# One plain column instead of two ahead of the seven-product columns in an encoder's feed-forward

## The chip, the cores and the metric

The kernel runs on one core of a Trainium2 chip. The metric is device time in microseconds (us) of the whole program; the time before is 2812.5 us, the median of three runs. Five engines work side by side, each through its own fixed list of instructions: PE (TensorE, matrix products into PSUM banks), DVE (VectorE), ACT (ScalarE), POOL (GpSimd) and SP (SyncE, which here issues the data transfers).

## The reference, cut to what matters

A two-layer encoder trunk is applied to a prompt of 256 tokens and a sample of 1024 tokens, all in float32, with a model width of 1024. Each layer has a mixer and then a feed-forward network with 2816 hidden values:

```
for i in range(DEPTH):                       # DEPTH = 2
    ...                                      # mixer: y
    x = x + g1 * rms_norm(y, norm_g[i, 1])
    h = rms_norm(x, norm_g[i, 2]) * (1 + sc2) + sh2
    a, bb = jnp.split(h @ ffn_w_in[i], 2, axis=-1)
    y = (jax.nn.silu(a) * bb) @ ffn_w_out[i]
    x = x + g2 * rms_norm(y, norm_g[i, 3])
```

The change lies in `h @ ffn_w_in[i]`, the first product of the feed-forward, once per layer.

## The kernel before, in words

**Blocks and precision.** The tokens lie in three blocks: A and B (512 sample tokens each) and C (256 prompt tokens). A float32 product is made of three fast matmuls: each operand is split into a high and a low part (`hi`, `lo`), and hi·hi, hi·lo and lo·hi are summed in PSUM. `hhi` and `hlo` hold these parts of the block's normalised values h, transposed, in 8 slices of 128 features.

**A plain column.** The hidden values are made in 22 columns j of 128. In a plain column (`plain`, L1236, with `mm3`, L299) the a half and the b half of the column are products of 8 slices x 3 = 24 matmuls for each block. `L1241` takes silu of the a half on ACT, `L1243` multiplies by the b half on DVE.

**A seven-product column.** In the other columns (loop at L1274, `seven`, L1224) A and B are multiplied together by a Strassen-Winograd scheme: the four block products of (A, B) with (a, b) are made of seven products of half depth, 12 matmuls each, while C stays plain. It needs sums of the blocks, T2, T3 and T4, and sums of the column's weights. `combos` (L1160) makes the block sums: 16 subtractions on DVE (L1164), then 16 splits, each a cast on ACT (L1157) and a subtraction on DVE (L1158), in the order hhiA/hloA, T2, T3, T4. `sums` (L164; L169 to L172) makes the weight sums, four DVE operations per column, and `parts` (L141, L142) splits them. The weight sums lie in the first half of the tile `both` (L1271), a buffer in which the last input of T4 lies until then. The seven products come in this order: two of block B with the weights' a half; C; T2 with the weight sums; A with the weight sums; T3; C; T4; the second half of A. The product with T4 adds into the bank that the sum at L1307 on DVE reads first.

**What comes ahead.** The values h of a block come out of `boundary` (L484): the sums of squares of the product before, eight additions of the old x on DVE (L507) with x loaded in pieces by SP (L490) into three buffers and the result stored (L511), a second norm with its small DVE rows (L466 to L472), four scalings on DVE (L520), and then `turn` (L524): for each of 8 slices four transposes on PE (L532), the high part on ACT (L535), the value on ACT (L540) or DVE (L538), the low part on DVE (L542). The blocks come in the order C, A, B, and plain columns of a block stand between the boundaries of the next (L1251 to L1267).

**What sets the order.** The kernel keeps lists of side work (`vec`, `fill`) and takes from them at each `tick` by the microseconds that it reckons for the products just issued; `drain_with` and `vec.drain` empty a list. A layer below then gives each engine a fixed list. An engine works through its list in order and waits at an instruction until its inputs are there.

**After the columns of a pair.** `rights` (L1181) stores and combines the four blocks of a pair of columns for the second product (SP stores at L1183, sums at L1189 to L1197); `lefts` (L1204) does the same for the second product's weights, in the second half of `both`.

Of the kernel before, what the change touches and what calls it, by code (L numbers as in the profile page):

```python
# [8 lines left out]
F32 = mybir.dt.float32  # L9
# [20 lines left out]
ORDER = ["C", "A", "B"]  # L30
DRING = 5
VR = 1.2
NPL = 2
NK = NH // 2
RUNS = "1674253"

# [2 lines left out]
def encoder_kernel(  # L39
# [19 lines left out]
    def nm(s):  # L59
        uid[0] += 1  # L60
        return f"{s}_{uid[0]}"
# [127 lines left out]
    class Work:  # L189
# [8 lines left out]
        def tick(self, us):  # L198
            self.credit += us
            while self.q and self.credit > 0:  # L200
                try:
                    self.credit -= next(self.q[0])
                except StopIteration:
                    self.q.pop(0)
            if not self.q:
                self.credit = 0.0
# [10 lines left out]
    vec = Work()  # L217
    fill = Work()

    def drain_with(gen, other):  # L220
        while gen in vec.q:
            vec.tick(1.0)
            if other is not None:
                next(other, None)
# [5 lines left out]
    def cols(w, m, width=128, k0=0, kn=KD):  # L230
        v = w.rearrange("(k p) m -> p k m", p=128)
        return v[:, k0 : k0 + kn, m : m + width]

    def spec_cols(key, w, c0):
        units.specs.append((key, cols(w, c0), 128))
# [25 lines left out]
    def spec_ffn(L):  # L261
        wi, wo = ffn_w_in[L], ffn_w_out[L]
        for j in range(NPL):
            spec_cols(("a", L, j), wi, j * 128)
            spec_cols(("b", L, j), wi, HID + j * 128)
        for j in range(NPL, NH):
            pair = (cols(wi, j * 128), cols(wi, HID + j * 128))
# [321 lines left out]
    with tc.tile_pool(name="st", bufs=1, reuse_waits="tile") as st:  # L589
# [61 lines left out]
        class ADP:  # L651
            i = 0
# [419 lines left out]
    bt = ctx.enter_context(tc.tile_pool(name="bt", bufs=2, reuse_waits="tile"))  # L1072
# [11 lines left out]
    def ypart(blk, h, dt=F32, shape=None):  # L1084
        return yp.tile(shape or [128, 4 if blk != "C" else KD, BLK[blk]], dt, tag=f"y{blk}{h}", name=nm("y"))
# [66 lines left out]
    def ffn_in(L, gens_in, fp, t_in):  # L1152
# [7 lines left out]
        def combos():  # L1160
            a0, a1, b0, b1 = v_of["A"] + v_of["B"]
            for i in range(4):
                for out, x, y in ((b0, a0, b0), (a0, a1, a0), (a1, a1, b0), (b1, b1, a1)):
                    dve.tensor_sub(out[:, i, :], x[:, i, :], y[:, i, :])  # L1164
                    yield 0.7
            for i in range(4):
                split_t(b0, hhi["A"][:, i, :], hlo["A"][:, i, :], i)
                yield 0.7
            T[2] = ypart("B", 0, F32R), ypart("B", 1, F32R)
            T[3] = ypart("A", 0, F32R), fp.tile([128, 4, 512], F32R, tag="t4l", name=nm("t3"))  # L1170
            for n, t in ((2, a1), (3, a0)):
                for i in range(4):
                    split_t(t, T[n][0][:, i, :], T[n][1][:, i, :], i)
                    yield 0.7
            T[4] = tuple(fp.tile([128, 4, 512], F32R, tag=t, name=nm("t4")) for t in ("t3l", "t3h"))
            for i in range(4):
                split_t(b1, T[4][0][:, i, :], T[4][1][:, i, :], i)
                yield 0.7


        def rights(k, a, b, c, d):  # L1181
            def put(o, t):
                dma(out=td[o][:, k, :], in_=t)  # L1183

            yield 3.0
            for o, t in (("1", a), ("2", c), ("3", d)):
                put(o, t)
            x = bt.tile([128, 512], F32, tag="r", name=nm("x"))
            dve.tensor_sub(x, b, a)  # L1189
            yield 1.4  # L1190
            dve.tensor_sub(b, d, b)
            yield 1.4
            put("5", x)
            dve.tensor_add(a, b, a)
            yield 1.4
            put("7", b)
            dve.tensor_sub(c, a, c)  # L1197
            yield 1.4
            put("6", a)
            yield 1.4  # L1200
            put("4", c)


        def lefts():  # L1204
            w = ffn_w_out[L].rearrange("(k t p) (h c) -> k p t h c", t=2, p=128, h=2)
            for k in range(NK):
                for c0 in (0, 256):
                    t = both[:, 2:4, :].rearrange("p i (u c) -> p (i u) c", u=2)
                    for i in range(2):
                        dma(out=t[:, 2 * i : 2 * i + 2, :], in_=w[k][:, i, :, c0 : c0 + 256])  # L1210
                    yield 12.0
                    dve.tensor_add(t[:, 3, :], t[:, 1, :], t[:, 3, :])
                    dve.tensor_sub(t[:, 1, :], t[:, 0, :], t[:, 1, :])
                    yield 1.0
                    dve.tensor_sub(t[:, 0, :], t[:, 3, :], t[:, 0, :])
                    dve.tensor_sub(t[:, 2, :], t[:, 2, :], t[:, 0, :])
                    yield 6.0
                    dma(out=s_dr[L][:, k, :, c0 : c0 + 256], in_=t)
                    yield 1.0
# [16 lines left out]
        def plain(blk, j, w, part, s):  # L1236
            n = BLK[blk]
            ps = (ps_mm() if part == 0 or blk != "C" else ps_ax())[:, :n]
            mm3(ps, w, blk)
            if part == 0:  # L1240
                act.activation(s, ps, AF.Silu)  # L1241
            else:
                dve.tensor_mul(s, s, ps)  # L1243
                if blk == "C":
                    store_c(j, s)

        first = ypart("C", 0, F32, [128, 4, 512])
        place = {"A": first[:, 0:2, :], "B": first[:, 2:4, :]}

        ua, ub = [], []  # L1250
        for ib, blk in enumerate(ORDER):  # L1251
            us_ = 5.4 * BLK[blk] / 512
            drain_with(gens_in[blk], None)
            if blk == "B":
                vec.push(combos())
            for j in range(NPL):
                if ib == 0:
                    ua.append(units.next(("a", L, j), 2))
                    ub.append(units.next(("b", L, j), 1))
                if blk == "C":  # L1260
                    s = bt.tile([128, 256], F32, tag="accC", bufs=1, name=nm("gc"))
                else:
                    s = place[blk][:, j, :]
                plain(blk, j, ua[j], 0, s)
                tick(us_, 0.8)
                plain(blk, j, ub[j], 1, s)
                tick(us_, 0.8)  # L1267
        vec.push(rights(0, *(first[:, i, :] for i in (0, 2, 1, 3))))
        vec.drain()
        units.spare = lambda: ypart("C", 0, F32R, [128, 2, 1024])  # L1270
        both = ypart("A", 1)  # L1271
# [1 line left out]
        fill.push(lefts())  # L1273
        for j in range(NPL, NH):  # L1274
            last = j == NH - 1
# [52 lines left out]
            else:  # L1328
                even = ga, gb
# [135 lines left out]
    rights = Rights(0)  # L1465
    with tc.tile_pool(name="f0", bufs=1, reuse_waits="tile") as fp:
        gens = out_proj("go", 0, 0, fp)
        units.ahead(3)
        ffn_in(0, gens, fp, rights.upto)
# [200 lines left out]
    rights = Rights(1)  # L1670
    with tc.tile_pool(name="f1", bufs=1, reuse_waits="tile") as fp:
        gens = out_proj("so", 1, 2, fp)
        units.ahead(3)
        ffn_in(1, gens, fp, rights.upto)
# [35 lines left out]
```

## Time and profile before

| | |
|---|---|
| median of 3 runs | 2812.5 us (2806.85 to 2815.17) |
| the profiled execution | 2806.46 us, span 2804.8 us |
| mean granted TensorE clock | 0.995 |
| PE busy | 2744.8 us (98%) |
| DVE busy | 1652.8 us (59%) |
| ACT busy | 1117.7 us (40%) |
| moved by DMA | 410.41 MB, mean 146 GB/s |
| instructions | 37193 |

In rows of the trace the first number is the start in us from the beginning of the span, the second the length in us; then engine, line, operation, output<-inputs and the number of instructions merged into the row. What stands in brackets is the idle time of the engine just before and what ended it. Starts of successive rows on one engine lie a little closer than their lengths, since an instruction's end overlaps the next one's start; matmuls overlap most.

### The profile page before, as it was taken

The page shows a single profiled execution, that of the slowest core. Times are in us where ns is not written, and L with a number is a line of the kernel's source. Part 1 is how long each engine was busy: PE and PEld are TensorE (multiplying, and loading weights), DVE is VectorE, ACT ScalarE, POOL GpSimd, SP SyncE. Part 2 cuts the span into 40 slices and gives each one's busy share as a digit, 9 for nine tenths or more (in the row PEclk, how much of TensorE's full clock was granted, in tenths as well). Part 3 has the DMA queues.
Part 4 walks back from the last instruction along what each step waited for, and adds up shares of the span by engine and source line. Part 5 has one row for each costly group of instructions (what it writes and reads, how often), then busy time and mean ns, then how long its engine had stood idle before and what let it go on. Part 6 is the DMA issues. An engine that isn't in the chain of part 4 may idle for free.

```text
span 2804.8 us, 37193 instructions
## 1 busy us (share of the span) xinstructions
PE 2744.8 (98%) x14328; PEld 2273.6 (81%) x14328; DVE 1652.8 (59%) x2669; ACT 1117.7 (40%) x1892; POOL 31.9 (1%) x43
## 2 busy tenths in 40 slices
PE   7999999999999999999999999999999999999998
PEld 4987888866888888888878868878887888888886
DVE  6663646554866654545577677636856555445576
ACT  5442434433632222334456434525522232224443
POOL 0000000000000000000000000000000000000000
PEclk9999999999999999999999999999999999999999
DMA  6224232256255542237676353334345532237576
GB/s 233 66 66 149 74 109 68 64 193 195 91 186 174 182 132 85 87 98 240 190 253 221 113 169 117 123 121 139 107 158 183 183 101 89 81 114 256 189 242 210
DMA packets 317542, 410.41 MB, mean 146 GB/s; under 512 B 21058, under 2 KB 194820, under 8 KB 317364
## 3 DMA queue, kind: packets, MB, share of 16 engines
q1 hardware_dynamic: 317364, 408.04, 44.8%
q8 instruction: 112, 1.84, 0.3%
q14 instruction: 66, 0.54, 0.1%
HBM read 304.65 MB, written 103.32 MB: 145 GB/s over the span
## 4 chain that ended last, share of the span: by engine, by line
PE 76%; DMA 10%; DVE 9%; issue 2%; ACT 1%; SPq 1%; POOL 0%; DVEq 0%; ACTq 0%; POOLq 0%
PE pso L1230 10%; PE pmm L1230 5%; PE pmm L318 4%; DMA y<-in_ffn_w_out_dram 3%; PE pax L1230 3%; PE pso L1404 3%; PE pso L1405 3%; PE pso L1403 3%; PE pax L344 2%; PE pmm L305 2%; PE pmm L304 2%; PE pmm L303 2%; DMA raw<-in_ffn_w_in_dram 2%; PE pso L1116 2%; PE pso L1118 2%
## 5 line engine op out<-in xcount | busy, mean ns | idle before, releaser
L141 ACT CAST uhi<-raw 128x1024 fp32r<-128x1024 f32 (+1 forms) x299 | 307.5, 1030 | 643.1 <-issue 276.3
L142 DVE TENSOR_TENSOR ulo<-raw,uhi 128x1024 fp32r<-128x1024 f32 (+1 forms) x299 | 357.9, 1199 | 260.2 <-ACT uhi L141 258.3
L305 PE MATMUL pax<-hhiC,ulo 128*128 128x256 f32 x680 | 192.6, 283 | 0.0
L304 PE MATMUL pax<-hloC,uhi 128*128 128x256 f32 x680 | 192.4, 283 | 0.0
L303 PE MATMUL pax<-hhiC,uhi 128*128 128x256 f32 x680 | 192.3, 283 | 0.0
L1230 PE MATMUL pso<-t,uhi 128*128 128x512 f32 x428 | 147.1, 405 | 17.0 <-DVE c L1307 17.0
L1403 PE MATMUL pso<-uhi,hhiB 128*128 128x512 f32 x374 | 145.0, 390 | 1.2 <-ACT hhiB L1352 1.0
L1404 PE MATMUL pso<-uhi,hloB 128*128 128x512 f32 x374 | 145.6, 389 | 0.2 <-DVE hloB L1353 0.2
L1405 PE MATMUL pso<-ulo,hhiB 128*128 128x512 f32 x374 | 145.6, 389 | 0.0
L1353 DVE TENSOR_TENSOR hloB<-tl,hhiB 128x512 fp32r<-128x512 f32 x154 | 104.3, 689 | 49.4 <-ACT hhiB L1352 49.0
L303 PEld LDWEIGHTS pax<-hhiC,uhi 128*128 128x128 f32 x680 | 130.2, 191 | 3.4
L304 PEld LDWEIGHTS pax<-hloC,uhi 128*128 128x128 f32 x680 | 130.2, 191 | 3.1
L305 PEld LDWEIGHTS pax<-hhiC,ulo 128*128 128x128 f32 x680 | 130.2, 191 | 1.7 <-issue 1.7
L1352 ACT CAST hhiB<-tl 128x512 fp32r<-128x512 f32 x154 | 94.3, 619 | 85.3 <-PE pso L1405 39.5
L1230 PE MATMUL pso<-y,uhi 128*128 128x512 f32 x324 | 109.2, 391 | 0.0
L1230 PEld LDWEIGHTS pso<-t,uhi 128*128 128x128 f32 x428 | 79.5, 193 | 34.8 <-DVE c L1307 19.3
L1403 PE MATMUL pmm<-uhi,hhiB 128*128 128x512 f32 x242 | 94.7, 391 | 1.0 <-ACT hhiB L1352 1.0
L1404 PE MATMUL pmm<-uhi,hloB 128*128 128x512 f32 x242 | 94.3, 390 | 0.2 <-DVE hloB L1353 0.2
L1405 PE MATMUL pmm<-ulo,hhiB 128*128 128x512 f32 x242 | 94.2, 389 | 0.0
L169 DVE TENSOR_TENSOR y<-raw 128x512 f32<-128x512 f32 x40 | 27.7, 693 | 104.4 <-DMA raw<-in_ffn_w_in_dram 104.3
L344 PE MATMUL pax<-wada,sct 128*2 128x512 f32 x384 | 84.2, 598 | 1.6 <-DMA wada<-in_w_ada_dram 1.2
L1230 PE MATMUL pmm<-hloA,uhi 128*128 128x512 f32 x216 | 84.3, 390 | 0.0
(457 smaller groups left out, 7223.2 us busy)
## 6 DMA issues: line engine op xcount, KB each, us to landing
wada<-in_w_ada_dram SPq DMA_DIRECT2D x96, 512.0 KB
raw<-in_ffn_w_in_dram SPq DMA_DIRECT2D x88, 512.0 KB
tl<-tdr SPq DMA_DIRECT2D x154, 256.0 KB
raw<-in_ffn_w_out_dram SPq DMA_DIRECT2D x74, 512.0 KB
y<-in_ffn_w_out_dram SPq DMA_DIRECT2D x88, 256.0 KB
sdr<-y SPq DMA_DIRECT2D x44, 512.0 KB
raw<-sdr SPq DMA_DIRECT2D x40, 512.0 KB
tdr<-c SPq DMA_DIRECT2D x60, 256.0 KB
```

Of the source, the lines that this page charges most:

```text
L141: act.copy(hi[:, :n], raw[:, :n])
L142: dve.tensor_sub(lo[:, :n], raw[:, :n], hi[:, :n].bitcast(F32))
L303: pe.matmul(ps, lhsT=hi[:, c], rhs=hhi[blk][:, k, :], start=(k == 0), stop=False)
L304: pe.matmul(ps, lhsT=hi[:, c], rhs=hlo[blk][:, k, :], start=False, stop=False)
L305: pe.matmul(ps, lhsT=lo[:, c], rhs=hhi[blk][:, k, :], start=False, stop=(k == KD - 1))
L318: pe.matmul(ps, lhsT=l, rhs=r, start=(i == 0), stop=(i == 3 * KD - 1))
L344: pe.matmul(ps[p0 : p0 + 2, :], lhsT=sct[:, :, k], rhs=raw[:, q * 512 : (q + 1) * 512], start=(k == 0), stop=(k == KD - 1), tile_position= ...
L1230: pe.matmul(ps, lhsT=l[:, c], rhs=r[:, k, :], start=start, stop=(k == 3 and l is lo), skip_group_check=True)
L1353: dve.tensor_sub(lo, t, hi.bitcast(F32))
L1403: pe.matmul(ps, lhsT=th[:, t], rhs=hi[:, c], start=(k == 0), stop=False)
L1404: pe.matmul(ps, lhsT=tl[:, t], rhs=hi[:, c], start=False, stop=False)
L1405: pe.matmul(ps, lhsT=th[:, t], rhs=lo[:, c], start=False, stop=(k == NK - 1))
```

## The change

`NPL`, the number of plain columns, goes from 2 to 1. So column 0 alone is plain, and columns 1 to 21 are made by seven products. Before, columns 0 and 1 were a pair of their own, with their four blocks in the tile `first` and a `rights` right behind them. Now the A and B blocks of column 0 lie in two tiles of the kind that later even columns use (`even`), and column 1 pushes the pair's `rights` at its own end. The weights' list (`spec_ffn`, L261) follows `NPL`. Bytes loaded and stored stay the same.

```
-NPL = 2
+NPL = 1
...
-        first = ypart("C", 0, F32, [128, 4, 512])
-        place = {"A": first[:, 0:2, :], "B": first[:, 2:4, :]}
-
+        even = [bt.tile([128, 512], F32, tag="acc" + x, bufs=1, name=nm("g0")) for x in "AB"]
...
                 else:
-                    s = place[blk][:, j, :]
+                    s = even[blk == "B"]
...
-        vec.push(rights(0, *(first[:, i, :] for i in (0, 2, 1, 3))))
         vec.drain()
```

What this does to the engines' lists is shown at three places of layer 0; layer 1 has the same rows there. The first is DVE from the end of the mixer's output product of block B to block B's first addition of x. `hloA` rows belong to the turn of block A, `m`, `tt` and `rt` to block B's norm, `ulo` to weight splits, `gc` to C's plain column. Before:

```order
L142 TENSOR_TENSOR ulo_6381<-raw_6378,uhi_6380 128x1024
L1142 TENSOR_TENSOR y_5343<-pmm_6229,gate_5336 128x512
L538 TENSOR_SCALAR v_6220<-pax_6258,mods_83 128x512
L542 TENSOR_TENSOR hloA_89<-v_6220,hhiA_86 128x512 x2
L538 TENSOR_SCALAR v_6220<-pax_6274,mods_83 128x512
L142 TENSOR_TENSOR ulo_6389<-raw_6384,uhi_6388 128x1024
L542 TENSOR_TENSOR hloA_89<-v_6220,hhiA_86 128x512
L466 TENSOR_TENSOR m_6459<-ss_5346 128x4
L467 TENSOR_SCALAR m_6459<-m_6459 128x4
L542 TENSOR_TENSOR hloA_89<-v_6221,hhiA_86 128x512
L1243 TENSOR_TENSOR gc_6300<-gc_6300,pax_6336 128x256
L469 TENSOR_TENSOR tt_6461<-rt_6460 128x4
```

Now, over the same stretch:

```order
L1142 TENSOR_TENSOR y_5343<-pmm_6229,gate_5336 128x512
L466 TENSOR_TENSOR m_6420<-ss_5346 128x4
L538 TENSOR_SCALAR v_6220<-pax_6258,mods_83 128x512
L467 TENSOR_SCALAR m_6420<-m_6420 128x4
L542 TENSOR_TENSOR hloA_89<-v_6220,hhiA_86 128x512 x2
L538 TENSOR_SCALAR v_6220<-pax_6274,mods_83 128x512
L469 TENSOR_TENSOR tt_6422<-rt_6421 128x4
L542 TENSOR_TENSOR hloA_89<-v_6220,hhiA_86 128x512
L470 TENSOR_TENSOR tt_6422<-m_6420,tt_6422 128x4
L471 TENSOR_SCALAR tt_6422<-tt_6422 128x4
L472 TENSOR_TENSOR rt_6421<-rt_6421,tt_6422 128x4
L507 SCALAR_TENSOR_TENSOR y_5342<-y_5342,rt_6421,xk_6390 128x512
```

Block B's norm has moved ahead, the two weight splits are gone from the stretch, and C's product comes after the additions begin.

The second place is DVE from the splits of T3 (`t_1241` before, `t_1229` now) to the split of the first weight sums. Before, with the rows of the first pair's `rights` (`x_6859`, `y_6299`) among them:

```order
L1158 TENSOR_TENSOR t_1241_6829<-v_6220,y_6828 128x512 x4
L1189 TENSOR_TENSOR x_6859<-y_6299 128x512
L1158 TENSOR_TENSOR t_1243_6847<-y_6607,t_1242_6846 128x512 x2
L1243 TENSOR_TENSOR y_6299<-y_6299,pmm_6798 128x512
L1158 TENSOR_TENSOR t_1243_6847<-y_6607,t_1242_6846 128x512 x2
L1191 TENSOR_TENSOR y_6299<-y_6299 128x512
L169 TENSOR_TENSOR y_6868<-raw_6386 128x512
L1194 TENSOR_TENSOR y_6299<-y_6299 128x512
L170 TENSOR_TENSOR y_6868<-y_6868,raw_6384 128x512
```

Now:

```order
L1158 TENSOR_TENSOR t_1229_6660<-v_6220,y_6659 128x512 x4
L1281 TENSOR_TENSOR c_1241_6706<-c_1241_6706,pax_6705 128x512
L1158 TENSOR_TENSOR t_1231_6678<-y_6516,t_1230_6677 128x512 x4
L169 TENSOR_TENSOR y_6687<-raw_6295 128x512
L170 TENSOR_TENSOR y_6687<-y_6687,raw_6293 128x512
L171 TENSOR_TENSOR raw_6293<-raw_6293,raw_6295 128x512
L172 TENSOR_TENSOR raw_6293<-raw_6293,y_6687 128x512
L142 TENSOR_TENSOR ulo_6693<-y_6687,uhi_6692 128x1024
```

The weight sums (`y_6868` before, `y_6687` now) still stand behind the last split of T4; the rows of `rights` have left the stretch, and the first sum of a seven-product column (`c_1241`, the line called L1281 now and L1284 before) stands inside it.

The third place is PE behind block A's plain products, where block B's transposes (`pax`, of `y_5342` and `y_5343`) and its plain products (`pso_6581` the a half, `pmm_6614` the b half) begin. Now:

```order
L532 MATMUL pax_6517<-ident,y_5343 128x128
L532 MATMUL pax_6525<-ident,y_5343 128x128
L532 MATMUL pax_6533<-ident,y_5343 128x128
L303 MATMUL pso_6581<-hhiB_87,uhi_6283 128x512
L303 MATMUL pmm_6614<-hhiB_87,uhi_6289 128x512
L1230 MATMUL pso_6704<-hhiB_87,uhi_6297 128x512
L532 MATMUL pax_6541<-ident,y_5342 128x128 x2
L532 MATMUL pax_6541<-ident,y_5343 128x128 x2
L304 MATMUL pso_6581<-hloB_90,uhi_6283 128x512
```

Before, the first slice's transposes stood in the middle of block A's products, and the list at this place held the a half of one column alone; now the a half, the b half and the first seven-product (`pso_6704`, L1230) take turns as slices of B come in.

## The prediction

> **What bounds the kernel now.** I read the page first, then PE's waits, then the first product's opening by stages, then each engine's rows there.
>
> ```profile
> PE 2744.8 (98%) x14328; PEld 2273.6 (81%) x14328; DVE 1652.8 (59%) x2669; ACT 1117.7 (40%) x1892; POOL 31.9 (1%) x43
> ```
>
> ```profile
> PE pso L1230 <- DVE c L1307: 17.0, 11, 3.6
> ```
>
> PE is the bound, and waits little. Inside the seven-product columns it waits 17.0 us in 11 waits for DVE at L1307. In the stretch of the change, by stages (columns: length, then busy us of PE, PE's weight loads, DVE, ACT, POOL, then clock and DMA):
>
> ```profile
> 706.70:720.20 13.50, 13.50 (x116) 13.50 (x115) 11.57 (x23) 13.41 (x21) 0.00 (x0) 1.00 0.50 154
> 720.20:742.50 22.30, 22.30 (x103) 18.38 (x102) 12.42 (x23) 10.20 (x22) 0.00 (x0) 1.00 0.43 140
> 742.50:767.60 25.10, 25.10 (x124) 20.70 (x123) 25.03 (x41) 16.05 (x27) 0.00 (x0) 1.00 0.03 11
> 767.60:775.90 8.30, 8.30 (x49) 7.36 (x48) 8.30 (x13) 4.23 (x5) 0.00 (x0) 1.00 0.64 219
> ```
>
> These are layer 0's plain columns of C, of A, of B, and the first three products of column 2. PE never waits, but DVE is full too from 742.5 on, though only 59% busy over the span. So the plain products are a cover: under them DVE and ACT finish blocks A and B, the sums of the blocks and the first weight sums. The cover fits to the microsecond: DVE's split of the weight sums ends at 773.93 + 1.24 = 775.2, and PE first uses it at 776.39.
>
> ```profile
> 705.26 0.69 DVE L542 TENSOR_TENSOR hloA<-v,hhiA 128x512 fp32r<-128x512 f32 x1
> ...
> 715.59 0.75 DVE L507 SCALAR_TENSOR_TENSOR y<-y,rt,xk 128x512 f32<-128x512 f32 x1
> ...
> 728.53 0.75 DVE L507 SCALAR_TENSOR_TENSOR y<-y,rt,xk 128x512 f32<-128x512 f32 x1 [0.55 <-DMA xk<-in_x_sample_dram]
> ...
> 732.92 2.74 DVE L520 TENSOR_SCALAR y<-y,rt 128x1024 f32<-128x1024 f32 x4
> ...
> 750.35 0.80 DVE L538 TENSOR_SCALAR y<-pax,mods 128x512 f32<-128x512 f32 x1
> 751.07 0.68 DVE L1164 TENSOR_TENSOR y<-y,v 128x512 f32<-128x512 f32 x1
> 751.67 0.68 DVE L542 TENSOR_TENSOR hloB<-y,hhiB 128x512 fp32r<-128x512 f32 x1
> 768.51 1.30 DVE L1158 TENSOR_TENSOR t<-y,t 128x512 fp32r<-128x512 f32 x2
> ...
> 770.32 0.70 DVE L169 TENSOR_TENSOR y<-raw 128x512 f32<-128x512 f32 x1
> ...
> 773.93 1.24 DVE L142 TENSOR_TENSOR ulo<-y,uhi 128x1024 fp32r<-128x1024 f32 x1
> 775.06 2.37 DVE L142 TENSOR_TENSOR ulo<-raw,uhi 128x1024 fp32r<-128x1024 f32 x2
> ```
>
> ```profile
> 744.97 1.46 ACT L535 ACTIVATE hhiB<-pax,mods 128x512 fp32r<-128x512 f32 x2
> 746.30 0.80 ACT L540 ACTIVATE y<-pax,mods 128x512 f32<-128x512 f32 x1
> ...
> 772.26 1.05 ACT L141 CAST uhi<-y 128x1024 fp32r<-128x1024 f32 x1 [1.14 <-DVE y L170]
> ```
>
> ```profile
> 776.39 0.39 PE L1230 MATMUL pso<-y,ulo 128*128 128x512 f32 x1
> ```
>
> Start to start in these rows, a 512-wide sum or split on DVE takes 0.60 us, a scale from PSUM (L538) 0.72, a weight split 1.13, a full-width scaling 0.68; on ACT a row of the turn takes 0.66.
>
> **What the change saves on PE.** Twelve matmuls in a row take 2.72 us, a C product of 24 takes 2.95, and a whole seven-product column 24.94, from one column's copy to the next:
>
> ```profile
> 767.77 2.72 PE pso L1230 x12
> ```
>
> ```profile
> 706.73 0.36 PE L303 MATMUL pmm<-hhiC,uhi 128*128 128x256 f32 x1
> ...
> 709.68 0.49 PE L532 MATMUL pax<-ident,y 128*128 128x128 f32 x3
> ```
>
> ```profile
> 1202.54 0.59 ACT L1281 COPY c<-pso 128x512 f32<-128x512 f32 x1 [0.74 <-PE pso L1230]
> ...
> 1227.48 0.59 ACT L1281 COPY c<-pso 128x512 f32<-128x512 f32 x1 [1.05 <-PE pso L1230]
> ```
>
> A plain column is 2 x 2.95 + 4 x 5.44 = 27.66 us. The exchange saves 2.72 us per layer, 5.4 us in both, if PE still never waits. Transfers keep their bytes and DMA stands at 0.03 in B's stage, so I cost them at nothing beyond the places below. On DVE a seven-product column has 4 sums and two weight splits more than a plain one, 4 x 0.60 + 2 x 1.13 = 4.7 us, and the first pair's `rights`, four sums (2.4 us), move into column 2; both fall behind the stretch, into columns in which PE takes 24.94 us and DVE isn't full (59% over the span). If that cover failed, it would show at L1307, step (6).
>
> **What it uncovers.** Without waits PE would now be through the plain column at 706.7 + 60.9 - 27.7 = 739.9, and through the first two half-depth products and C at 739.9 + 8.4 = 748.3. There it needs the weight sums. DVE's chain, followed in its new order:
>
> (1) From hloA to block B's first addition stand L1142, three hloA, two scales and six 4-wide rows of the norm (0.2 each, an estimate: a third of a 512-wide row's): 0.6 + 1.8 + 1.4 + 1.2, and 0.4 for ACT's value, so 711.3 instead of 715.6.
>
> (2) Three additions run at once; the others wait for x. From SP's issue to DVE's use it took 3.43 us once and 4.33 us once:
>
> ```profile
> 716.76 0.42 SPq L490 DMA_DIRECT2D xk<-in_x_sample_dram  x1
> ...
> 722.90 0.40 SPq L490 DMA_DIRECT2D xk<-in_x_sample_dram  x1
> ```
>
> ```profile
> 720.19 0.75 DVE L507 SCALAR_TENSOR_TENSOR y<-y,rt,xk 128x512 f32<-128x512 f32 x1 [0.60 <-DMA xk<-in_x_sample_dram]
> ...
> 727.23 0.75 DVE L507 SCALAR_TENSOR_TENSOR y<-y,rt,xk 128x512 f32<-128x512 f32 x1 [1.62 <-DMA xk<-in_x_sample_dram]
> ```
>
> With three buffers, load 4 follows addition 1, addition 4 (716) frees load 7, and addition 5, behind three rows of block A, comes at 718.5 and frees load 8 at 719.6. I take 3.6 us, near the shorter, since one weight load instead of three goes out beside it: last addition at 723.4; with 4.33 it is 724.1. SP has C's store (L1234) ahead of load 5, which waits for DVE's product; that fits within addition 5's time.
>
> (3) From last addition to scalings it took 732.92 - 728.53 = 4.4, and PE's b half of A, for which DVE now waits in between, ends at about 726 (706.7, plus 5.9 for C, 13.5 - 11.8 = 1.7 of transposes as in the first stage before, 10.9 for A, and 0.8 for A's last low part, which stands behind addition 5): scalings from 727.8, over at 730.5. PE, out of work at 726, waits about 5 us here.
>
> (4) The turn of B: ACT's first two rows and the transposes, 1.8; then eight low parts, four scales and three block sums on DVE, 8 x 0.6 + 4 x 0.72 + 3 x 0.6 = 9.5: over at 741.8 (before, 752.3). ACT's twelve rows, 7.9 us, run beside it. PE feeds on slices as they come and ends B's products at about 745, which hides under (5).
>
> (5) Thirteen block sums, one product with the b half, sixteen splits and the sum for column 1: 31 x 0.60 = 18.6, over at 760.4. The weight sums can't be earlier: they lie where T4's input lay. Two sums and ACT's cast take it to 762.7, the split to 764.0.
>
> PE, there at 748.3, does three matmuls on the high part and stands: 15.0 us of waits per layer, (3)'s among them.
>
> (6) Column 1's sixth product waits for L1307. Ahead of it DVE needs column 2's second weight tile; its buffer comes free behind the split at 766.3.
>
> ```profile
> 776.33 1.51 SPq L130 DMA_DIRECT2D raw<-in_ffn_w_in_dram  x2
> ```
>
> ```profile
> 780.21 0.69 DVE L169 TENSOR_TENSOR y<-raw 128x512 f32<-128x512 f32 x1 [0.25 <-DMA raw<-in_ffn_w_in_dram]
> ...
> 785.57 0.68 DVE L1307 TENSOR_TENSOR c<-c,pso 128x512 f32<-128x512 f32 x1
> ```
>
> ```profile
> 2027.57 0.74 PE L1230 MATMUL pso<-t,uhi 128*128 128x512 f32 x2 [0.91 <-DVE c L1307]
> ```
>
> Issue to use took 3.9 us: sums from 770.3, then as before 785.6 - 780.2 = 5.4 to L1307, which ends at 776.3. PE is there at 764.0 + 4.8 + 2.7 + 2.95 = 774.4: 1.9 us of wait. Before, layer 0 had no wait here and layer 1 had 0.91, which goes.
>
> Sum: layer 0, 15.0 + 1.9 - 2.7 = +14.2; layer 1, whose lists are alike, +13.3; together +27.5. The profiled execution took 2806.46 us (span 2804.8), so 2834; it lay 6 under the median of the runs, 2812.5, against which I forecast 2840.
>
> **A rule weighed.** The trace has one wait of PE of 3.6 us, and the clock column behind it:
>
> ```profile
> 26.70:30.30 3.60, 0.00 (x0) 0.00 (x1) 3.18 (x6) 3.05 (x5) 0.00 (x0) 1.00 1.09 391
> 34.00:35.00 1.00, 1.00 (x7) 0.88 (x6) 0.73 (x2) 0.56 (x1) 0.00 (x0) 0.50 0.57 209
> 37.00:38.00 1.00, 0.72 (x4) 0.00 (x0) 0.96 (x3) 0.00 (x0) 0.00 (x0) 0.81 0.03 8
> ```
>
> The clock was half some 7 us. If it halves behind my waits too, up to 3.5 us are lost behind each: the 1.9 of (6) hides part of the second, and DVE waits for B's late b half for at most 2. That adds 0 to 3.6 per layer; I take 0 and keep 7. The Trainium skill, "TensorE: Matmul & The Clock Gate", Part 1, says that the clock halves after an idle window of about 3.4 us and returns after as much sustained work. The trace agrees on the half, not on the time. By it each of the two waits would lose an estimated 1.7 us, nearly all of it under the 1.9 of (6) and the wait for the weight sums, and the sum would end at an estimated 2841.
>
> **The rivals.** *DVE without waits* (0.14): its rows from 705.9 to the split of the weight sums add up to 49.6 us by the steps above, so 755.5 at the earliest; PE then waits 6.5, +3.8 a layer, 2819. For it: DVE was full behind 742.5. Against: x must still be loaded. Halfway is 2829.
>
> *Slower loads and clock* (0.18): loads of 4.33 us or worse and half clock, up to +5.5 a layer: 2846 to 2852.
>
> *The column waits go* (0.06), the faster side: the 17.0 us at L1307. PE's late start could put it behind DVE for good. This decides if the two new waits stay under 5.4 + 17.0 = 22.4 us; their floor is 13, giving 2803, while with my waits it ends at 2824. Against: they come in later columns, from `lefts` and its loads, which start anew.
>
> **How the numbers follow.** The forecast, 2834 to 2846, has 0.62. The range, 2824 to 2853, leaves out the lower half of the DVE rival and most of the last. A measurement tells about 0.3%, 8 us. Faster 0.03 (column waits and floor together), same 0.06 (the DVE floor and mixes), slower 0.91.
>
> **What would show it.** PE idle about 5 us ahead of B's first product and about 10 us ahead of the first product with T2, releaser DVE or ACT of the weight sums; column 1's first copy near 748; DVE full from about 731 to 764; L1307 waits up by 2 to 4. I am wrong if PE reaches T2 later than DVE's split, or if PE's new waits are under 10 us in all.

## The result, and the profile after

The changed kernel takes 2853.7 us (median of 4 runs, 2846.4 to 2854.2) against 2811.8 us before (4 runs). The ratio is 1.0151, 95% interval 1.0136 to 1.0166. Run again later beside the kernel before, it stood at 1.0138 (1.0118 to 1.0159). It is slower, as forecast, but by some 38 to 42 us instead of 28, and the 2853.7 us lie just outside the range of 2824 to 2853. The profiled execution took 2846.4 us (span 2844.7), 39.9 above that of before.

The engines' line and PE's waits of the changed kernel:

```profile
PE 2757.2 (97%) x14304; PEld 2280.1 (80%) x14304; DVE 1668.8 (59%) x2687; ACT 1122.8 (39%) x1898; POOL 31.5 (1%) x43
```

```profile
PE pso L1230 <- ACT uhi L141: 19.5, 2, 9.7
PE pso L1230 <- DVE c L1304: 14.9, 9, 2.9
PE pax L532 <- DVE y L520: 9.0, 4, 2.5
...
PE pso L1400 <- ACT hhiB L1349: 2.4, 1, 2.4
PE pmm L1400 <- ACT hhiB L1349: 1.9, 1, 1.9
```

The first row is new: in each layer PE stands 9.7 us ahead of its first product on T2, until the weight sums are cast. The third had 3.8 us in 2 waits; two of 2.4 have joined it, ahead of block B's transposes. The waits inside the columns (L1304, before L1307) are no larger than they were.

PE has 24 matmuls fewer and yet is busy 12.4 us longer. The clock says why: by the trace's clock PE lost 26.0 us to half speed while it was busy, against 8.8 before, and these 17.2 us less 5.4 for the 24 matmuls come to 11.8. Layer 0's opening by stages (length, then PE, its weight loads, DVE, ACT and POOL, then clock and DMA):

```profile
726.03:728.61 2.58, 0.16 (x1) 0.03 (x1) 2.24 (x7) 0.84 (x2) 0.00 (x0) 1.00 0.28 106
728.61:732.00 3.39, 2.67 (x13) 1.56 (x14) 1.84 (x3) 1.01 (x2) 0.00 (x0) 0.79 0.02 7
732.00:736.00 4.00, 4.00 (x12) 3.11 (x13) 3.53 (x6) 3.14 (x5) 0.00 (x0) 0.50 0.00 0
736.00:740.00 4.00, 4.00 (x25) 3.66 (x24) 2.08 (x4) 2.91 (x5) 0.00 (x0) 0.82 0.00 0
740.00:756.00 16.00, 16.00 (x84) 13.67 (x82) 15.58 (x26) 8.72 (x14) 0.00 (x0) 1.00 0.00 1
756.00:760.00 4.00, 0.15 (x2) 0.00 (x0) 4.00 (x8) 4.00 (x9) 0.00 (x0) 1.00 0.00 0
760.00:764.00 4.00, 0.00 (x0) 0.00 (x0) 3.96 (x7) 0.73 (x2) 0.00 (x0) 0.66 0.00 0
764.00:768.00 4.00, 2.11 (x5) 1.47 (x6) 3.93 (x6) 3.21 (x4) 0.00 (x0) 0.50 0.39 131
768.00:772.00 4.00, 4.00 (x12) 3.14 (x11) 3.90 (x6) 0.84 (x2) 0.00 (x0) 0.56 0.55 154
772.00:776.00 4.00, 4.00 (x19) 3.24 (x18) 3.23 (x7) 3.01 (x5) 0.00 (x0) 1.00 0.77 256
```

Read three things here. PE is empty twice (726.0 to 728.6, and 756.1 to 765.9). Behind each hole the clock stands at half for some microseconds (6.8 us from 730.6 on, and 5.6 us of work from 765.9 on), in which 12 matmuls go through in 4 us (732 to 736) where the last stage has 19. And DVE is full through the second hole: PE waits for it.

The chain on DVE, row by row, with the steps of the prediction in order: first x-addition, last x-addition, scalings, last low part of block B, the product with B's late half, T4's splits, weight sums, their split, and the addition that releases column 1's sixth product:

```profile
711.12 2.08 DVE L507 SCALAR_TENSOR_TENSOR y<-y,rt,xk 128x512 f32<-128x512 f32 x3
...
723.80 0.75 DVE L507 SCALAR_TENSOR_TENSOR y<-y,rt,xk 128x512 f32<-128x512 f32 x1 [1.30 <-DMA xk<-in_x_sample_dram]
...
727.71 0.75 DVE L520 TENSOR_SCALAR y<-y,rt 128x1024 f32<-128x1024 f32 x1
...
743.46 0.68 DVE L542 TENSOR_TENSOR hloB<-y,hhiB 128x512 fp32r<-128x512 f32 x1
...
748.17 0.69 DVE L1243 TENSOR_TENSOR g<-g,pmm 128x512 f32<-128x512 f32 x1 [0.42 <-PE pmm L305]
...
760.82 2.49 DVE L1158 TENSOR_TENSOR t<-y,t 128x512 fp32r<-128x512 f32 x4
763.34 0.69 DVE L169 TENSOR_TENSOR y<-raw 128x512 f32<-128x512 f32 x1
...
766.00 1.22 DVE L142 TENSOR_TENSOR ulo<-y,uhi 128x1024 fp32r<-128x1024 f32 x1
...
778.22 0.68 DVE L1304 TENSOR_TENSOR c<-c,pso 128x512 f32<-128x512 f32 x1
```

PE's two waits and the start of its sixth product in column 1, then ACT waiting for a half-clock transpose:

```profile
728.61 2.77 PE L532 MATMUL pax<-ident,y 128*128 128x128 f32 x12 [2.42 <-DVE y L520]
...
765.89 1.22 PE L1230 MATMUL pso<-y,uhi 128*128 128x512 f32 x2 [9.74 <-ACT uhi L141]
...
779.79 0.63 PE L1230 MATMUL pso<-t,uhi 128*128 128x512 f32 x2
```

```profile
736.92 0.78 ACT L535 ACTIVATE hhiB<-pax,mods 128x512 fp32r<-128x512 f32 x1 [1.78 <-PE pax L532]
```

To see where the 39.9 us arise, compare the first copies of the columns. In the changed kernel columns 1 and 2 of layer 0 begin at

```profile
750.63 0.58 ACT L1278 COPY c<-pso 128x512 f32<-128x512 f32 x1
...
788.70 0.58 ACT L1278 COPY c<-pso 128x512 f32<-128x512 f32 x1
```

and before, columns 2 and 3 at

```profile
770.52 0.59 ACT L1281 COPY c<-pso 128x512 f32<-128x512 f32 x1 [4.36 <-PE pso L1230]
...
795.84 0.57 ACT L1281 COPY c<-pso 128x512 f32<-128x512 f32 x1
```

Column 1 takes 788.70 - 750.63 = 38.1 us where a column without waits takes 24.9. By column 2 layer 0 is 788.70 - 770.52 = 18.2 us late. From column 12 on it is constantly 16.5 late. Layer 1's last columns are 36.7 late, so 20.2 more, and the remaining 3.2 come behind them: at 2566.4, in layer 1's second product, PE waits 2.4 us (an L1400 row) where it waited 1.0 before, and 3.4 us at half clock follow. In the second profile of the same kernel (below) the three parts are 17.6, 13.2 and 1.4, together 32.2. So a few microseconds of each layer are a matter of the run, which the experiments place.

### The profile page after: what moved, and what is told of

Its sections match the earlier page's. It is cut to its first block, busy times and chain, and to the rows that moved or that the text cites. A ratio compares the mean times of both kernels' runs of the same rounds, so it can differ in the third digit from the quotient of the medians.

```text
span 2844.7 us, 37176 instructions
## 1 busy us (share of the span) xinstructions
PE 2757.2 (97%) x14304; PEld 2280.1 (80%) x14304; DVE 1668.8 (59%) x2687; ACT 1122.8 (39%) x1898; POOL 31.5 (1%) x43
## 3 DMA queue, kind: packets, MB, share of 16 engines
q8 instruction: 112, 1.84, 0.3%
## 4 chain that ended last, share of the span: by engine, by line
PE 77%; DMA 10%; DVE 9%; issue 2%; ACT 1%; SPq 1%; POOL 0%; DVEq 0%; ACTq 0%; POOLq 0%
PE pso L1230 13%; PE pmm L1230 6%; PE pmm L318 4%; PE pax L1230 3%; PE pso L1400 3%; PE pso L1402 3%; PE pso L1401 3%; PE pax L344 2%; PE pax L305 2%; PE pax L304 2%; PE pax L303 2%; DMA y<-in_ffn_w_out_dram 2%; PE pmm L303 2%; PE pmm L304 2%; PE pmm L305 2%; PE pso L1116 2%
## 5 line engine op out<-in xcount | busy, mean ns | idle before, releaser
L1230 PE MATMUL pso<-t,uhi 128*128 128x512 f32 x448 | 155.6, 409 | 14.9 <-DVE c L1304 14.9
L1400 PE MATMUL pso<-uhi,hhiB 128*128 128x512 f32 x374 | 145.3, 391 | 2.9 <-ACT hhiB L1349 2.4
L1230 PE MATMUL pso<-y,uhi 128*128 128x512 f32 x336 | 116.8, 403 | 19.5 <-ACT uhi L141 19.5
L1230 PEld LDWEIGHTS pso<-t,uhi 128*128 128x128 f32 x448 | 84.6, 196 | 33.4 <-DVE c L1304 16.7
L1400 PE MATMUL pmm<-uhi,hhiB 128*128 128x512 f32 x242 | 94.9, 392 | 2.0 <-ACT hhiB L1349 1.9
L169 DVE TENSOR_TENSOR y<-raw 128x512 f32<-128x512 f32 x42 | 29.1, 692 | 115.4 <-DMA raw<-in_ffn_w_in_dram 115.3
L1230 PEld LDWEIGHTS pso<-y,uhi 128*128 128x128 f32 x336 | 63.3, 195 | 32.2 <-ACT uhi L141 19.9
L1230 PE MATMUL pso<-y,ulo 128*128 128x512 f32 x224 | 88.8, 396 | 0.0
```

The lines of the kernel that those rows point to most:

```text
L1230: pe.matmul(ps, lhsT=l[:, c], rhs=r[:, k, :], start=start, stop=(k == 3 and l is lo), skip_group_check=True)
L1400: pe.matmul(ps, lhsT=th[:, t], rhs=hi[:, c], start=(k == 0), stop=False)
```

## The experiments

My theory after the result: the plain column was cover for one chain (block B's x-additions, its turn, the sums of the blocks, T2 to T4, the weight sums). Its end is set by DVE, and each of the two holes halves PE's clock; the first half-clock stretch also delays the chain itself, since the transposes and B's products feed it. Rivals: what exceeds the forecast is a price of the new column count itself, paid in later columns and across layers; or the clock is harmless, because PE would wait for DVE anyway.

Three lengths, read from the timelines, tell the kernels apart better than their totals. For layer 0 / layer 1, in us: from A's last plain product to the first product on T2 (changed kernel, layer 0: 765.89 - 725.80); from there to column 2's copy (788.70 - 765.89); and what columns 2 to 10 take above nine times 24.93 (1019.62 - 788.70 - 224.37).

| kernel | A's end to T2 | T2 to column 2 | columns 2 to 10, excess |
|---|---|---|---|
| changed | 40.1 / 39.6 | 22.8 / 23.1 | 6.5 / 16.8 |
| changed, again | 38.5 / 39.8 | 22.2 / 22.6 | 10.6 / 9.0 |
| e3: T2's wait filled | 39.7 / 39.6 | 21.5 / 21.5 | 15.2 / 9.6 |
| e5: B's wait filled | 37.9 / 37.7 | 22.6 / 22.1 | 13.0 / 15.0 |
| e4: sums early | 36.9 / 37.8 | 19.8 / 19.8 | 11.4 / 7.1 |
| e9: sums on POOL, T2 first | 28.7 / 27.9 | 19.9 / 19.7 | 12.3 / 10.0 |
| e10: e9, B's wait filled | 28.2 / 28.9 | 19.9 / 19.6 | 5.4 / 9.3 |
| e12: sums held, T2 first | 30.2 / 30.2 | 20.0 / 19.9 | 14.2 / 21.5 |
| e13: e12, B's wait filled | 27.9 / 27.7 | 20.0 / 20.2 | 18.6 / 16.5 |

The kernel before has 8.9 / 15.5 in the last column, for the nine columns from its first of seven products on.

**The change in layer 0 alone.**

```diff
-NPL = 1
+NPLS = (1, 2)
...
-            for j in range(NPL):
+            for j in range(npl):
```

> The change in layer 0 alone; layer 1 keeps two plain columns. Theory (each layer pays for its own uncovered chain: in the changed kernel's trace layer 0's columns start 16.5 us later from column 12 on, layer 1 adds 20, the tail 3): +17 us over the kernel before, near 2829 us, layer 1's columns no further behind than layer 0's. Rival (the cost is a price of the different column count on the whole program, loads and stores that collide later): the second layer and the tail slip too, 2835 to 2845 us. Rival (layer 1 pays nearly all, layer 0's loss is caught up by its second product): 2812 to 2818 us.

2830.5 us against 2807.2 of the kernel before beside it: 1.0070 (1.0049 to 1.0091), +23, above the theory's 17. In its trace layer 0 ends its columns 23.6 us late, and layer 1 ends its own 23.6 late: layer 1 adds nothing, on balance, where it isn't changed (it begins 29.1 late and regains 5.5 through its columns). So each layer pays for itself, and the rival of a program-wide cost falls; the 6 us more than expected lie in layer 0's columns 2 to 10, whose excess is 12.3 here against 6.5.

**The changed kernel again**, unaltered.

> The changed kernel once more, as it is. Theory (its cost over the kernel before is fixed up to the first column of seven products and through it, 21 us per layer against 27.7 us of one plain column saved and 24.9 added; what columns 2 to 10 add over 24.93 us each is a matter of the run): first waits of 9.7 us and intervals of 38 us again, the sum of the excess over columns 2 to 10 other than the 6.7 and 16.7 us of the first profile by several us; 36 to 44 us above the kernel before. Rival (the later columns' excess is a fixed part of the change): 6.7 and 16.7 us again within 1 us.

2842.7 us against 2805.1, +37.6. Waits and column 1 repeat:

```profile
PE pso L1230 <- ACT uhi L141: 19.5, 2, 9.7
```

The excess of columns 2 to 10 doesn't (10.6 / 9.0). It varies between 6 and 17 us per layer in kernels that don't differ there, so a median says little about an edit worth 4 us, and the table's first two columns are the measure. In these two profiles the excess is PE's idle time plus half of each stretch at half clock: 4.6 + 1.7 and 10.2 + 6.8 us in the first, 7.2 + 3.4 and 8.1 + 0 in the second. So the waits and the clock behind them differ from run to run.

**T2's wait filled.** 36 matmuls whose result nobody reads, ahead of the product on T2.

```diff
+            if j == NPL:
+                warm = ps_ax()
+                for i in range(36):
+                    pe.matmul(warm, lhsT=hhi["A"][:, i % 4, 0:128], rhs=hhi["A"][:, i % 4, :], start=True, stop=True)
             seven(a, ws, 1, T[2], False)
```

> The changed kernel with 36 matmuls of 128x512 that nobody reads, ahead of the first product on T2 in each layer, where TensorE waits 9.7 us: the wait stays filled, so the clock is not halved behind it. Theory (the chain of VectorE ends the wait, and the half clock behind it is a cost of its own): the product on T2 starts where it did (765.9 us in layer 0) but the next 8 us run at full clock, 4 us earlier, of which up to 2 us are given back at the sixth product, which then waits for the addition at L1304: 2 to 4 us per layer, 2846 to 2850 us. Rival (the halved clock is all of the cost above the forecast): 2840 us. Rival (the clock costs nothing, VectorE's chain sets column 1 anyway): 2853 to 2855 us.

2846.5 us against 2807.2, 1.0128 (1.0108 to 1.0148). The total lies at the theory's low end, but the kernel before ran 5 us faster here, too, and against 1.0151 and 1.0138 that tells little. The stretch itself shows what happened (PE's waits from 726 to 790, then stages):

```profile
PE pax L532 <- DVE y L520: 2.5, 1, 2.5
PE pso L1230 <- ACT uhi L141: 1.6, 1, 1.6
```

```profile
760.00:768.00 8.00, 7.11 (x32) 5.56 (x30) 7.90 (x14) 3.95 (x8) 0.00 (x0) 1.00 0.04 7
768.00:772.00 4.00, 3.33 (x11) 2.57 (x12) 4.00 (x5) 3.47 (x4) 0.00 (x0) 0.80 0.37 117
772.00:776.00 4.00, 4.00 (x15) 3.15 (x14) 3.89 (x8) 1.61 (x2) 0.00 (x0) 0.77 0.90 265
```

The product on T2 comes no earlier (39.7 from A's end, against 40.1 and 38.5 in the two profiles without): the wait is DVE's. The clock behind it is better but not full: the filling ended 1.6 us too soon, and 3.4 us at half clock follow instead of 10.2. T2 to column 2 falls by 0.6 to 1.6 us, out of the 2.3 to 3.2 that it takes above the undisturbed 19.9.

**B's wait filled.** 18 such matmuls ahead of block B's first transposes.

```diff
+        if blk == "B" and not first:
+            warm = ps_ax()
+            for i in range(18):
+                pe.matmul(warm, lhsT=hhi["A"][:, i % 4, 0:128], rhs=hhi["A"][:, i % 4, :], start=True, stop=True)
         for k in range(KD):
```

> The changed kernel with 18 matmuls of 128x512 that nobody reads ahead of the first transposes of block B at the feed-forward boundary, where TensorE waits 2.4 us and then ran at half clock from 728 to 736 us. Theory (the half clock slows the transposes, these slow the turn of B and with it VectorE's chain): the turn ends at 742 instead of 744 us, the chain and the first product on T2 come 2 us earlier, 1.5 to 2.5 us per layer: 2848 to 2851 us. Rival (the turn is set by ACT and VectorE, not by the transposes): TensorE ends B's products 3 us earlier and waits 3 us longer ahead of T2: 2853 to 2855 us. Rival (every half-clock us counts in full): 3.4 us per layer, 2846 to 2847 us.

2847.1 us, 1.0127 (1.0105 to 1.0148); the total tells as little as e3's. But the stages from the filling on are at full clock, and the wait ahead of T2 is as long as ever:

```profile
728.13:732.00 3.87, 3.87 (x19) 3.21 (x18) 3.38 (x9) 1.00 (x2) 0.00 (x0) 1.00 0.24 92
732.00:736.00 4.00, 3.94 (x24) 2.87 (x23) 2.10 (x4) 2.87 (x5) 0.00 (x0) 1.00 0.00 0
736.00:740.00 4.00, 4.00 (x28) 3.42 (x26) 3.99 (x8) 4.00 (x7) 0.00 (x0) 1.00 0.00 0
```

```profile
PE pso L1234 <- ACT uhi L141: 9.7, 1, 9.7
```

From A's end to T2 it now takes 37.8 us (mean of the layers) instead of 39.8 and 39.1 in the two profiles without. So 1.3 to 2.0 us per layer were the clock's, as the theory said, and they came through the chain: PE is earlier, and DVE with it. The length goes with the half clock behind B's hole: 37.9 and 37.7 us with none (e5), 38.5 with 3.4 us of it (layer 0 of the repeat), 39.6 to 40.1 with 6.8 us (the other three). The link is the turn. In the changed kernel ACT waits 1.78 us for half-clock transposes (the row at 736.92 above), and DVE for ACT:

```profile
738.40 1.29 DVE L542 TENSOR_TENSOR hloB<-y,hhiB 128x512 fp32r<-128x512 f32 x2 [1.93 <-ACT y L540]
```

With the clock up DVE doesn't wait there, and the turn is over 16.5 and 16.3 us behind A's end instead of 18.3 and 18.1; from there to T2 it is 21.4 to 21.8 us in both kernels. A slow PE delays the engine for which PE then waits.

**The weight sums early.** Column 1's sums in a tile of their own, made ahead of the combinations.

```diff
             if blk == "B":
                 vec.push(combos())
+                units.sum_tile = lambda: ypart("C", 0, F32, [128, 2, 512])
+                units.ahead(3)
```

> The changed kernel with column 1's weight sums made in a tile of their own ahead of the combinations, no longer behind the splits of T4 on VectorE. Theory (the product on T2 waits for the sums, which wait for all 31 rows of the combinations): the product then needs T2 alone, 24 rows of 0.60 us behind the end of the turn (744.1 + 14.4 = 758.5 us) instead of 765.9; TensorE is there at 756: 6 to 8 us per layer less, 2838 to 2842 us. Rival (the four additions and the split, some 4 us of VectorE, only move ahead of the turn of B and delay it by as much): 3 to 4 us per layer, 2846 to 2848 us. Rival (the wait only moves on to T3 and T4 in the same column): 2850 to 2854 us.

2827.7 us, 1.0064 (1.0043 to 1.0085): 17 to 21 us off the changed kernel's +38 to +42, more than the 12 to 16 expected. Here are PE's waits from 700 to 800, and DVE's first x-addition:

```profile
PE pax L532 <- DVE y L520: 13.1, 2, 11.3
PE pso L1230 <- DVE c L1306: 1.1, 1, 1.1
```

```profile
716.94 1.42 DVE L507 SCALAR_TENSOR_TENSOR y<-y,rt,xk 128x512 f32<-128x512 f32 x2
```

The wait ahead of T2 is gone, and with it the half clock behind it (T2 to column 2: 19.8). The rival had half of it: the sums run ahead of B's x-additions, which start 5.8 us later, and PE's wait there grew from 2.4 to 11.3. Two waits became one, and one hole costs one half-clock stretch. The x-additions' rows, not the sums' own cost, are what to protect.

**Sums on POOL, T2 first.** The next kernels order the combinations so that T2 comes first (three block sums per slice, T2's splits, A's, T3's, then the fourth sums and T4's).

```diff
...
-                for out, x, y in ((b0, a0, b0), (a0, a1, a0), (a1, a1, b0), (b1, b1, a1)):
+                for out, x, y in ((b0, a0, b0), (a0, a1, a0), (a1, a1, b0)):
...
+            for i in range(4):
+                split_t(a1, T[2][0][:, i, :], T[2][1][:, i, :], i)
+                yield 0.7
...
+                units.sum_tile = lambda: ypart("C", 0, F32, [128, 2, 512])
+                units.eng = pool
+                units.ahead(3)
+                units.eng = dve
```

> The changed kernel with column 1's weight sums and their two low parts made on POOL ahead of block B, and the combinations in another order: twelve subtractions, then T2's splits, then A's, T3's and T4's (what is computed stays). Theory (the wait ahead of T2 is only order on VectorE: sums behind T4, T2 behind 24 rows): the product on T2 finds everything ready, 16 rows of 0.60 us behind the turn (744 + 9.6 = 754 us, TensorE comes at 756); the interval from column 1 to column 2 falls from 38.1 to 25 us in both layers, and the kernel stands 12 to 16 us above the kernel before instead of 40, what is left being block B's wait with its half clock and the tail. Rival (the wait moves on to T3, T4 or the sixth product): 22 to 30 us above. Rival (POOL's slower additions come too late for the product on T2): the product waits for POOL, 25 to 35 us above.

2828.6 us against 2808.1, 1.0074 (1.0061 to 1.0088): +20, a miss by 4 to 8. As expected nothing waits at T2 (28.7 / 27.9 from A's end, column 1 in 25 us). But A's plain products take 22.2 / 24.3 us from C's first product on, where the changed kernel needs 19.2 / 19.8. DVE's and POOL's rows there:

```profile
709.83 2.29 DVE L467 TENSOR_TENSOR m<-ss 128x4 f32<-128x4 f32 x1
...
714.81 1.80 DVE L470 TENSOR_TENSOR tt<-rt 128x4 f32<-128x4 f32 x1
```

```profile
709.71 2.40 POOL L143 TENSOR_TENSOR ulo<-y,uhi 128x1024 fp32r<-128x1024 f32 x1
714.18 2.41 POOL L143 TENSOR_TENSOR ulo<-raw,uhi 128x1024 fp32r<-128x1024 f32 x1 [2.08 <-ACT uhi L142]
```

```profile
720.79 0.66 PE L533 MATMUL pax<-ident,y 128*128 128x128 f32 x4 [2.47 <-DVE gc L1249]
```

Two 4-wide rows of DVE's norm, 0.16 us elsewhere, take 2.29 and 1.80 (1.63 and 1.84 in layer 1), and end when POOL's row ends. They hold up DVE's queue, and PE meets a new wait of 2.47.

**The same, with B's wait filled** as in e5.

> As the kernel with the sums on POOL and T2 first, and 18 matmuls of 128x512 that nobody reads ahead of block B's transposes in each layer, so that the clock stays up over that wait. Theory (the half clock behind B's wait costs 2 to 3.5 us per layer of its own once TensorE is nowhere else waiting for VectorE): 6 to 11 us above the kernel before, 4 to 7 below the same without them. Rival (the clock's cost is hidden in the turn, or the matmuls delay the transposes by as much): no difference from the same without them.

2821.2 us, 1.0049 (1.0037 to 1.0061): 7 us below e9, as the theory had it, and +13 against the kernel before, 2 above its figure. But the opening doesn't show the theory's cause: from A's end to column 2 it takes 48.1 / 48.6 us here and 48.6 / 47.6 in e9. The two profiled executions differ by 11.3 us, and 7.6 of these lie in columns 2 to 10, 2.3 in layer 1's A products. So that the total fell as forecast is luck as far as these traces go: why e10 is faster is not shown. This is the best of the kernels with one plain column, and it still loses to two.

**C's first product moved into B's wait.** Real work in place of the filling; its edit emits `mm3(pc, wa1, "C")` of column 1, and with it POOL's sums, ahead of block B's gathering.

> As the kernel with the sums on POOL and T2 first, and block C's first product of column 1 (24 matmuls of 128x256, 2.9 us) moved out of column 1 to the wait ahead of block B's transposes. Theory (real work in that wait saves its own 2.9 us and the half clock behind): 4 to 6 us per layer below the kernel with the sums on POOL, 1 to 6 us above the kernel before. Rival (TensorE comes 3 to 5 us earlier to T2 and waits there for VectorE, whose chain sets the end): 8 to 14 us above. Rival (with every wait covered the 2.7 us per layer that the change saves show): 2 to 6 us below the kernel before.

2826.2 us, 1.0061 (1.0048 to 1.0073): +18, above every expectation, and not told apart from e9 by the total. From A's end to column 2 it takes 42.5 / 42.7 us instead of e9's 48.6 / 47.6, which is the expected gain; but e9's loss in A's products stays (23.7 / 23.1). The profiled executions differ by 11.7 us (2820.7 against 2832.4), nearly all of it the opening's 11; but this one is the fastest of its five and e9's the second slowest, and why the medians lie only 2.4 apart I can't place.

**The kernel before with the edit of e9.**

> The kernel before (two plain columns) with the same edit as the kernel with the sums on POOL: sums of the first seven-product column on POOL ahead of block B, T2's splits first. Theory (there the second plain column's 27.7 us cover the chain, so nothing waits for T2 or the sums): within 4 us of the kernel before. Rival (the sums and the order cost it time there too, so that part of the gain is not the change's): 5 to 15 us below it. Rival (POOL's work or the earlier sums hinder VectorE's chain): 3 to 8 us above.

2819.9 us, 1.0043 (1.0028 to 1.0057): +12, where the theory had said nothing would happen. PE's waits from 700 to 800:

```profile
PE pso L1236 <- ACT uhi L142: 3.8, 1, 3.8
PE pso L1236 <- POOL ulo L143: 2.8, 1, 2.8
```

Under two plain columns the edit makes the sums the late ones, and POOL's split later still. No expectation had it so high. So the edit costs something of its own, and between the two kernels that both have it the change is worth 2828.6 - 2819.9 = 8.6 us of loss, not 40.

**The sums held on DVE until B's turn is over, T2 first**, so that nothing is pulled ahead of the x-additions.

```diff
...
+                units.gate = const.tile([128, 1], F32, tag="gate1", name=nm("one"))
+                dve.tensor_scalar(units.gate, hlo["B"][:, KD - 1, 0:1].bitcast(F32), 0.0, 1.0, ALU.mult, ALU.add)
+                units.sum_tile = lambda: ypart("C", 0, F32, [128, 2, 512])
+                units.ahead(2)
+                units.gate = None
```

> The changed kernel with T2's splits first among the combinations and column 1's weight sums on VectorE, held until the turn of block B is over by an addition that multiplies with a 1.0 made from its last row; nothing is then pulled ahead of B's x-additions, as it was in the runs with the sums early. Theory: the x-additions begin at 711 us again, the turn ends at 744, sums and T2 are through after some 20 rows (744 + 13.5 = 757 to 758 us), TensorE is there at 756: a wait of 2 us and perhaps the half clock behind it in place of 9.7, so the first column's interval falls from 38.1 to 27 to 30 us: 8 to 11 us per layer off the changed kernel, 18 to 24 us above the kernel before; with no wait at all 12 to 16. Rival (the wait moves on to T3 and T4, whose rows come later by the four of the sums): 28 to 34 us above.

2832.1 us against 2805.1, 1.0100 (1.0083 to 1.0117): +27, above the theory's 12 to 24. The opening does better than expected: 50.3 / 50.1 us from A's end to column 2 instead of 62.9 / 62.7, no wait over 1 us at T2. That is 25 us in both layers, and the total shows 11. The rest went in columns 2 to 10: 14.2 / 21.5. The longest wait there is PE's for DVE, and DVE's row ahead of it came behind a weight load:

```profile
PE pso L1239 <- DVE c L1318: 3.4, 1, 3.4
```

```profile
2074.48 0.69 DVE L171 TENSOR_TENSOR y<-raw 128x512 f32<-128x512 f32 x1 [0.97 <-DMA raw<-in_ffn_w_in_dram]
```

**The same with B's wait filled, and the kernel before with the held sums.**

> The same as the kernel with the held sums, and 18 matmuls of 128x512 that nobody reads ahead of block B's transposes. Theory (the half clock behind B's wait lengthens the turn by 2 us and B's products by 3): 3 to 6 us below the same without them, of which TensorE's part can be lost again to VectorE at T2; 14 to 20 us above the kernel before. Rival (once TensorE waits for VectorE at T2 only the 2 us of the turn count): 2 to 4 us for both layers. Rival (no effect): within 1.5 us of the same without them.

> The kernel before with the same edit, two plain columns kept. Theory (under the second plain column the chain is covered, and nothing is pulled ahead of B's x-additions): within 4 us of the kernel before, unlike the kernel before with the sums on POOL ahead of B, which lost 12 us at T2. Rival (any reordering of this chain costs the kernel before, too): 8 to 14 us above. Rival (the order was worth time there too): 4 to 8 us below.

The first: 2824.0 us, 1.0060 (1.0041 to 1.0080), +19 and 8 below e12, where 3 to 6 were expected; in the opening 2.2 per layer, and the turn is shorter by 1.8 and 2.2. Over the whole opening, from C's first product to column 2's copy, the kernel before takes 63.8 us, the changed one 82.1 / 82.5, e12 68.8 / 69.2 and e13 66.6 / 66.8. So the order of the chain and the filled hole take back 15.6 of the changed kernel's 18.5 us per layer. The second: 2816.5 us, 1.0043 (1.0028 to 1.0057), +11, a miss, and the first rival's figure: reordering the chain costs the kernel before, too (PE waits 2.4 and 2.3 us for the sums ahead of T2), and between e12 and this kernel the change costs 15.6 us. Why the kernels with held sums have more excess in columns 2 to 10 (14 to 22 us) isn't settled: PE's idle time and half of the half-clock stretches make 10.5 and 17.8 of e12's 14.2 and 21.5, and that they wait there behind weight loads is only what one row shows.

## Why the prediction was right in kind and short in size

The mechanism stands. Step (1), the first x-addition at 711.3: measured 711.12. Step (2), the last at 723.4 with loads of 3.6 us: 723.80. Step (3), scalings from 727.8 to 730.5: 727.71 to 730.45; the wait of about 5 us showed as 2.4 of named wait, and the rest as a stretch in which PE had only transposes. Ahead of T2 about 10 us: 9.74.

The step that failed is **A rule weighed**: "That adds 0 to 3.6 per layer; I take 0 and keep 7." The half clock was seen in the trace of before and priced at nothing, because its cost was to hide under the sixth product's wait and the wait for the sums. Neither hid all of it.

- In step (4) the turn was to be over at 741.8 and PE to end B's products "at about 745, which hides under (5)". At half clock the last low part ended at 744.1, and the last products ended near 748.1, where DVE waited for them. The turn took 13.7 us where the sum had 11.3, and 11.7 with the hole filled; the filling gave back 1.3 to 2.0 us per layer (e5). Step (5) inherits it: T4's splits end at 763.3, not 760.4, and the first product on T2 starts at 765.89, not 762.7.
- In step (6) PE was to reach the sixth product at 774.4 and wait 1.9 for DVE (776.3). At half clock it came at 779.8, behind DVE's row of 778.22, and didn't wait. The 1.9 became 22.8 - 19.9 = 2.9 of clock, 1.0 more: the clock's cost hid the wait, but was longer.
- Of T2's 3.2 us of lateness 2.4 are the turn's, and 0.8 lie between its end and T2 (21.7 us, against 20.9 in the sum). With the 1.0 that makes 4: layer 0 stands 18.2 us late at column 2, against the forecast's 14.2. Layer 1 begins 17.1 late (C's first product, 1963.34 against 1946.23) and its column 2 stands 35.9 late (2045.87 against 2010.02), so 18.7, against 14.2 as well, since the 0.91 that the sum took off in layer 1 lies behind this mark. In the repeat the two openings are 15.9 and 17.5 us longer than before; the shorter one has the shortest half clock.

The sum had 27.5. In the first profile the openings make 36.9 and the stretch behind the columns, which the sum didn't have, 3.2, of 39.9; in the repeat 33.4 and 1.4, of 32.2. So the openings are 1.7 to 4.5 us per layer longer than the sum had them, most of it the clock that was priced at nothing. The medians stand 41.9 and 37.6 above those of before; that is about what columns 2 to 10 vary by (23.3 and 19.6 us for both layers in two profiles of one kernel, 24.4 before).

The Trainium skill, "TensorE: Matmul & The Clock Gate", Part 1, says that the window over which activity is watched runs freely, so that the moment of a change depends on where in it the work falls. The traces agree: layer 0's hole of 2.42 us ahead of B was followed by 6.8 us at half clock in one profile of the changed kernel and by 3.4 in the other, and one of 2.46 us in e10, at 721.96, by none. At the second product one of 1.90, at 1298.46, left the stage around it at full clock:

```profile
1296.00:1300.00 4.00, 2.10 (x10) 1.40 (x9) 2.81 (x5) 2.67 (x5) 0.00 (x0) 1.00 0.82 292
```

The idle window of about 3.4 us that the prediction took from the Trainium skill is not what these traces show: the changed kernel's holes ahead of B were shorter, 2.4 to 2.5 us, and half clock followed.

The rivals: *DVE without waits* fails on the load waits (1.30 ahead of the last x-addition). *Slower loads and clock* was half right, by its clock; the loads were as taken (the last addition 0.4 us later). *The column waits go* fails: 17.0 us before, 14.9 and 15.3 in the two profiles after.

The saving of 2.72 us per layer is real, but no kernel here showed it as a gain: with T2's wait removed and B's filled (e10) the change still stands 13 us above.

## What to carry to other kernels

When work is removed that an engine did while another prepared its next input, price the chain that it covered row by row, and then price the clock behind each hole as a term of its own, also where the hole is only 2 us: slowed transposes and products delay the very chain that PE waits for. Before filling a hole, ask what stands in the queue ahead of its releaser; here the order alone (the sums behind T4's splits, T2 behind 24 rows) was worth 13 us of each layer's 18, while sums that ran too early moved the wait ahead of block B (11.3 us in e4). Compare parts of the timeline where totals vary by more than the edit is worth.

## What was not expected of the hardware

A wait of TensorE of 1.6 us, behind matmuls at full clock, was followed by 8 us at 0.80 and 0.77 (e3), and one of 1.9 us by none; the same hole of 2.42 us was followed by 6.8 us at half clock in one execution and by 3.4 in the next. A 4-wide addition of DVE took 2.29 us, instead of 0.16, while POOL worked on a 128x1024 difference, and ended with it (e9); a row that reads PSUM kept its time beside another of POOL's (0.69 at 709.23).
